# Wide and narrow products of a two-layer decoder trunk in another order, with later attention steps and squares on VectorE in the tail

## The chip, the cores and the metric

One core of a Trainium2 chip runs the kernel. The time is device time in microseconds (us) of one execution, and the reported number is the median of several executions: before the change 838.62 us, of three runs from 836.81 to 839.08.

Engines are named as in the profile: PE is TensorE (PEld its weight loads), DVE is VectorE, ACT is ScalarE, POOL is GpSimd, SP is SyncE, which here only issues DMAs.

## What is computed

Two decoder layers on 256 tokens of width 2048, in fp32. Layer 0 mixes tokens by forgetting attention (FoX, 32 heads of 64, a learned decay added to the logits), layer 1 by sliding-window attention with grouped keys, learned sinks and partial rotation. Each layer projects the normalised input to q, k, v and a gate, multiplies the attention output by silu(gate), projects back and adds the residual. A last RMSNorm ends it.

```python
def reference(x, norm_g, fox_w_in, fox_b_f, fox_w_out, swa_w_in, swa_sinks, swa_w_out, final_g):
    ...
    for i in range(DEPTH):
        h = rmsnorm(x, norm_g[i])
        j = i // N_MIXERS
        if i % N_MIXERS == 0:
            p = h @ fox_w_in[j]
            ...
            y = fox_attention(q, k, v, log_f)
            w_out = fox_w_out[j]
        else:
            p = h @ swa_w_in[j]
            ...
            y = swa_attention(q, k, v, swa_sinks[j])
            w_out = swa_w_out[j]
        y = y * jax.nn.silu(gate)
        x = x + y @ w_out
    return rmsnorm(x, final_g)
```

## The kernel before

**Products.** Every operand of a projection is split into a high part (rounded to fp32r) and a low part (the rest). For weights this is a cast on ACT (L218) and a subtract on DVE (L219), four k-tiles of 128 rows at a time. A projection's 256 output columns are a `Unit`; its 16 k-tiles come in *parts* of four, and each part is worked in two blocks, one for each half `c` of the output columns (or of the tokens, for a `v` unit). A block of four k-tiles is four *wide* matmuls (high weights held, high and low activations moved together, 512 columns) and then four *narrow* ones (low weights held, high activations moved, 256 columns). Both add into the PSUM tile `acc`, whose two halves ACT (L282, a copy of the second) and DVE add together when the unit is finished. That is the unit's `consume`: for q and k it also scales and splits (`q` L513, L514, L342, L343; `k` L519, L520, L524 to L528), for the gate it goes on to silu (L308, L309, L296 to L303).

**Order.** PE's instructions stay in program order. The loop at the end of `trunk` goes through the stream of all parts, and each iteration runs block 0 of this part and then block 1 of the part before. Weights are fetched by SP three parts ahead into raw buffers, and the cast of a part waits until one of the five `w` buffers is free, which is when the last matmul that uses it is done.

**Attention by steps.** After every second matmul of a block `tick()` counts a step, eight in an iteration, and runs what is due then. The attention of a finished group is hung on these steps by `attend`, counted from when its `k` (or, in layer 1, its `q`) is consumed. A FoX group has two pairs of heads. For each pair: at `s - BIAS` the bias is asked for (a DMA by POOL, L567, and POOL's `affine_select`, L126), at step `s` comes a first score product (`ps_s`, keys of both blocks) with its bias add and reduction on DVE (L378, L365), at `s + SECOND` the second product (the first block of queries; `s_first`, L390, L365) and the softmax: two small operations on DVE (L579, L580), four exponentials on ACT (L321), reciprocal and four multiplies on DVE (L329, L332). At step `t` and `t + 4` PE transposes the two heads' weights (`pt`, L82), and at a last step come the products with `v` (`psy`). The score tiles share one PSUM buffer (`ps_s`, one buffer), so a score product waits until the reduction of the one before is done.

The steps stand in five tables: `FOX_FIRST` for group 0, `FOX_NEXT` for group 1, `FOX_ODD` for groups 3 and 5, `FOX_DUE` for 2, 4, 6 and 7, and `SWA_DUE` for the eight groups of layer 1. After an even FoX group's `k` come its gate (consumed 32 steps later), the next group's `q` (64 steps) and `k` (96). Odd groups have a `v` unit for two groups there, in 512 columns.

**Tail.** The last projection is worked half by half of the tokens; `finish` adds the residual, takes the sum of squares of the last two column blocks, works out the scale, spreads it over the partitions by a matmul with a diagonal matrix (`rows`), multiplies (L754) and sends the output in five pieces.

Of the kernel before, what the change touches and what calls it, by code (L numbers as in the profile page):

```python
# [48 lines left out]
KBUFS = 1  # L49
# [8 lines left out]
def trunk(  # L58
# [19 lines left out]
    def mm(*args, **kw):  # L78
        tc.keep_in_program_order(nc.tensor.matmul(*args, **kw))  # L79
# [142 lines left out]
    def block(unit, p, c):  # L222
        _, _, _, kt0, s = unit.parts[p]
        w, a = loaded[unit, p], unit.acts
        if p == 0 and (c == 0 or unit.apart):

            pool, tag, banks = unit.apart if c == 1 else (*unit.acc, 2)
            ps = pool.tile([P, banks, 512], F32, tag=tag, name="acc")
            if unit.apart:
                unit.ps[c] = ps[:, 0, :]  # L230
            else:
                unit.ps, unit.both = [ps[:, i, :] for i in range(2)], ps
        n = unit.n if unit.kind == "tok" else S
# [10 lines left out]
        ops = [operands(i) for i in range(s)]  # L244
        if unit.halves:

            for i, (sh, _, mv) in enumerate(ops):
                mm(both, sh, mv.rearrange("p h n -> p (h n)"), start=first and i == 0, stop=False)
                if i % 2:
                    tick()  # L250
            if s % 2:
                tick()
            for i, (_, sl, mv) in enumerate(ops):
                mm(ps, sl, mv[:, 0, :], start=False, stop=last and i == s - 1)
                if i % 2:
                    tick()
        elif n == 512:
            for i, (sh, sl, mv) in enumerate(ops):
                mm(ps, sh, mv[:, 0, :], start=first and i == 0, stop=False)
                mm(ps, sh, mv[:, 1, :], start=False, stop=False)  # L260
                tick()
                mm(ps, sl, mv[:, 0, :], start=False, stop=last and i == s - 1)
                tick()
        else:
            for i, (sh, sl, mv) in enumerate(ops):
                mm(ps, sh, mv[:, 0, :], start=first and i == 0, stop=False)
                mm(ps, sl, mv[:, 0, :], start=False, stop=False)
            for i, (sh, _, mv) in enumerate(ops):
                mm(ps, sh, mv[:, 1, :], start=False, stop=last and i == s - 1)
                tick()  # L270
        if p == len(unit.parts) - 1:
            if unit.apart:
                unit.consume(c, both)
            elif c == 1 and unit.kind == "tok":
                for i in range(2):
                    unit.consume(i, unit.ps[i])
            elif c == 1:
                unit.consume(unit.both)

    def low_half(ps):  # L280
        s = work.tile([P, 2, S], F32, tag="half", name="half", bufs=HALVES)
# [64 lines left out]
    class Pair:  # L346
# [92 lines left out]
    class Group:  # L439


        def attend(self, kt, due, shared):
            self.pts = [None, None]
            for j, (s, t, *second) in enumerate(due[0:2]):
                self.pair(j).later(self, s, t, *(second or [SECOND]))
            after(due[2], lambda: self.values(kt, shared))

        def values(self, kt, shared):
# [218 lines left out]
    def to_layer1(m):  # L667
        split_x(m, 1)
        square_into(sums1, m)
        if m == KT - 1:  # L670

            def norm():
                nonlocal swa
                fox_scope.__exit__(None, None, None)
                swa = ctx.enter_context(tc.tile_pool(name="swa", bufs=2))
                state["r1"] = r = inv_rms(
                    sums1, "n1", True, ps_s.tile([P, 2, 512], F32, tag="S", name="ps_n1")[:, 0, :]
                )
# [43 lines left out]
    def finish(th, ps):  # L722
# [2 lines left out]
        nc.vector.tensor_add(x, ps[:, 0 : 2 * P], x)  # L725
# [4 lines left out]
        nc.scalar.activation(sq, x, AF.Square, accum_out=ss)  # L730
        nc.scalar.activation(r, ss, AF.Ln, scale=1.0 / D, bias=tail["ss"][:, th : th + 1])
        nc.scalar.activation(r, r, AF.Exp, scale=-0.5)
        nc.vector.tensor_scalar(
            v, ss, 1.0 / D, tail["ss"][:, th : th + 1], op0=ALU.mult, op1=ALU.add
        )

        nc.vector.scalar_tensor_tensor(out=w, in0=r, scalar=-0.5, in1=r, op0=ALU.mult, op1=ALU.mult)
        nc.scalar.activation(diag, ident, AF.Copy, scale=r)
        nc.vector.tensor_scalar(w, w, v, 1.5, op0=ALU.mult, op1=ALU.add)
        nc.vector.tensor_scalar_mul(diag, diag, w)  # L740
        nc.vector.tensor_mul(r, r, w)

        def scale():
            rows = ps_s.tile([P, 2, 512], F32, tag="S", name="rows")[:, 0, :]
# [188 lines left out]
    sink = cpool.tile([P, H], F32, name="sink")  # L933
    state["sink"] = sink

    prev = None
    for i, (u, p) in enumerate(stream):
        fetch(i + 1 + LOOK)
        if u is last_out[7]:
            if p == 0:  # L940
                block(*prev, 1)
            block(u, p, 0)
            continue
        block(u, p, 0)
        if prev is not None:
            block(*prev, 1)
        prev = (u, p)
    for p in range(len(last_out[7].parts)):
        block(last_out[7], p, 1)


# ---- launch: one core; the host only lays arrays out
# [62 lines left out]
```

## Time and profile before

| | before |
|---|---|
| median of 3 runs | 838.62 us |
| the profiled execution | 838.05 us |
| its span | 836.3 us |
| mean granted PE clock | 0.995 |
| instructions in the span | 12770 |
| HBM traffic | 147.50 MB read, 2.15 MB written |

The profiled execution's own time is 1.75 us more than its span, which goes from the first to the last instruction on record. The profile's page gives busy time for each engine; matmuls are pipelined, so a busy PE only says that there was always a matmul in its pipe. The waits view names, for each engine, what the instruction waited for that ended an idle time; the chain is followed back from the last instruction; the timeline lists instructions by start time (us from the start of the span), with the idle time before them and its releaser in brackets.

### The profile page before, as it was taken

To read this page: it belongs to the slowest core of one execution; us is meant where nothing else is said; L and a number is where in the kernel's file an instruction comes from. 1 tells how busy PE (TensorE), PEld (TensorE's weight loads), DVE (VectorE), ACT (ScalarE), POOL (GpSimd) and SP (SyncE) were. 2 spreads that over 40 slices of the span, in tenths; PEclk is the share of its full clock that TensorE was granted. 3 is DMA by queue.
4 is the path that set the end of the run, shared out by engine and by line. 5 is a ranking of instruction groups with operands and counts; after the bars stand their busy time and mean duration, and the time that the engine had idled before them with its cause. 6 is when DMAs were issued, how large, how long until landed. Compare 5 with 4: busy or idle time off the path is not lost.

```text
span 836.3 us, 12770 instructions
## 1 busy us (share of the span) xinstructions
PE 822.7 (98%) x4778; PEld 708.7 (85%) x4778; DVE 644.8 (77%) x1201; ACT 519.6 (62%) x936; POOL 60.9 (7%) x93
## 2 busy tenths in 40 slices
PE   8999999999999999999999999999999999999995
PEld 7888788888888888888888888888888888888885
DVE  6898866887679866798659768788998888875654
ACT  6686665764666665576646556477667766765552
POOL 1011010010101010020002110000000000001210
PEclk9999999999999999999999999999999999999998
DMA  8667564555646555554374564544455435346622
GB/s 281 241 229 246 173 207 164 185 206 170 212 160 196 185 199 188 172 188 171 130 251 164 198 201 158 196 159 152 144 170 181 151 120 185 115 142 207 205 95 102
DMA packets 28399, 150.48 MB, mean 180 GB/s; under 512 B 3457, under 2 KB 5665, under 8 KB 14513
## 3 DMA queue, kind: packets, MB, share of 16 engines
q1 hardware_dynamic: 25920, 142.22, 50.0%
q0 software_dynamic: 1408, 6.36, 2.1%
q10 hardware_dynamic: 1008, 1.07, 0.4%
q8 instruction: 38, 0.62, 0.3%
q14 instruction: 25, 0.20, 0.1%
HBM read 147.50 MB, written 2.15 MB: 179 GB/s over the span
## 4 chain that ended last, share of the span: by engine, by line
PE 90%; DVE 4%; issue 3%; ACT 1%; DMA 1%; SPq 0%; POOL 0%; DVEq 0%; ACTq 0%; POOLq 0%
PE acc L79 82%; PE ps_s L79 3%; PE pt L82 2%; PE psy L79 2%; DVE w L219 1%; DVE q L343 1%; ACT w L218 1%; DMA wraw<-in_vf_dram 1%; SPq L210 0%; DVE xs L160 0%; DVE ys L462 0%; ACT st L321 0%; DVE st L365 0%; DVE scaled L754 0%; DVE st L332 0%
## 5 line engine op out<-in xcount | busy, mean ns | idle before, releaser
L79 PE MATMUL acc<-xs,w 128*128 128x256 f32 (+1 forms) x2624 | 485.6, 340 | 0.1
L79 PEld LDWEIGHTS acc<-xs,w 128*128 128x128 f32 x2624 | 406.8, 189 | 59.8 <-issue 3.4
L219 DVE TENSOR_TENSOR w<-wraw,w 128x1024 fp32r<-128x1024 f32 (+4 forms) x275 | 326.0, 1191 | 97.2 <-ACT w L218 95.1
L218 ACT CAST w<-wraw 128x1024 fp32r<-128x1024 f32 (+4 forms) x275 | 278.4, 1016 | 146.6 <-PE acc L79 107.0
L79 PE MATMUL acc<-ys,w 128*128 128x512 f32 x960 | 171.4, 338 | 0.0
L79 PEld LDWEIGHTS acc<-ys,w 128*128 128x128 f32 x960 | 147.6, 189 | 21.5 <-issue 0.4
L79 PE MATMUL acc<-w,xs 128*128 128x512 f32 (+2 forms) x512 | 111.4, 364 | 1.6 <-ACT w L218 1.3
L79 PEld LDWEIGHTS acc<-w,xs 128*128 128x128 f32 x512 | 86.8, 189 | 16.0 <-ACT w L218 1.6
L282 ACT COPY half<-acc 128x512 f32<-128x512 f32 x56 | 32.7, 583 | 81.4 <-PE acc L79 81.0
L321 ACT ACTIVATE st<-st,mx 128x128 f32<-128x128 f32 (+1 forms) x128 | 56.6, 445 | 2.4 <-DVE mx L827 1.6
L401 ACT COPY pts<-pt 128x384 f32<-128x384 f32 x64 | 30.4, 475 | 13.7 <-PE pt L82 12.9
L332 DVE TENSOR_SCALAR st<-st,rl 128x128 f32<-128x128 f32 (+1 forms) x128 | 32.9, 321 | 1.1
L79 PE MATMUL ps_s<-kk,q 128*128 128x256 f32 (+1 forms) x160 | 32.0, 310 | 1.8 <-DVE mx L365 1.1
L82 PE MATMUL pt<-ident,st 128*128 128x128 f32 x192 | 31.9, 274 | 0.3 <-DVE st L332 0.3
L661 POOL TENSOR_TENSOR acc<-acc,sq 128x256 f32<-128x256 f32 x28 | 24.5, 875 | 88.6 <-ACT sq L655 87.5
L365 DVE CUSTOM_DVE_ANT_0 st<-ps_s,st 128x128 f32<-128x128 f32 (+1 forms) x96 | 28.3, 331 | 1.1
L82 PEld LDWEIGHTS pt<-ident,st 128*128 128x128 f32 x192 | 23.5, 140 | 6.4 <-ACT half L282 0.7
L126 POOL TENSOR_SCALAR_AFFINE_SELECT bc<-bc 128x256 f32<-128x256 f32 x32 | 22.0, 706 | 74.6 <-DMA bc<-negc_d 74.6
L79 PEld LDWEIGHTS ps_s<-kk,q 128*128 128x128 f32 x160 | 23.4, 188 | 4.2 <-issue 1.5
L659 POOL COPY acc<-sq 128x256 f32<-128x256 f32 x2 | 1.3, 672 | 329.8 <-ACT sq L655 329.8
L567 POOL DMA_DIRECT2D bc<-negc_d x16 | 8.8, 553 | 213.7 <-DVE mx L365 186.3
L321 ACT ACTIVATION_READ_ACCUMULATOR st<-st,mx 128x1 f32 x128 | 24.2, 189 | 0.0
(139 smaller groups left out, 530.4 us busy)
## 6 DMA issues: line engine op xcount, KB each, us to landing
wraw<-in_fox_in_dram SPq DMA_DIRECT2D x46, 1024.0 KB, 5.0
wraw<-in_swa_in_dram SPq DMA_DIRECT2D x36, 1024.0 KB, 5.0
wraw<-in_fox_in_dram SPq DMA_DIRECT2D x28, 512.0 KB, 4.8
wraw<-in_fox_out_dram SPq DMA_DIRECT2D x13, 1024.0 KB, 5.0
wraw<-in_swa_out_dram SPq DMA_DIRECT2D x13, 1024.0 KB, 5.1
bc<-negc_d POOLq DMA_DIRECT2D x16, 384.0 KB, 5.3
wraw<-in_fox_out_dram SPq DMA_DIRECT2D x6, 512.0 KB, 3.6
wraw<-in_swa_out_dram SPq DMA_DIRECT2D x6, 512.0 KB, 3.6
```

The lines of the kernel that those rows point to most:

```text
L79: tc.keep_in_program_order(nc.tensor.matmul(*args, **kw))
L82: tc.keep_in_program_order(nc.tensor.transpose(out, in_, ident))
L126: return nc.gpsimd.affine_select(out=ap, in_=ap, compare_op=ALU.is_ge, fill=NEG, base=base, pattern=pattern, channel_multiplier=mult,)
L218: state["split"] = nc.scalar.copy(high, raw)
L219: nc.vector.tensor_tensor(out=low, in0=raw, in1=high.bitcast(F32), op=ALU.subtract)
L282: nc.scalar.copy(s, ps[:, :, S : 2 * S])
L321: nc.scalar.activation(st[:, hh, rng], st[:, hh, rng], AF.Exp, bias=nm[:, qb, hh : hh + 1], accum_out=l[:, qb, hh : hh + 1],)
L332: nc.vector.tensor_scalar_mul(st[:, hh, rng], st[:, hh, rng], rl[:, qb, hh : hh + 1])
L365: nc.vector.tensor_tensor_reduce(out=st, in0=high, in1=st, scale=self.scale, scalar=LOWEST, op0=ALU.add, op1=ALU.max, accum_out=self.mx[:, ...
L401: nc.scalar.copy(group.pts[hh][:, self.j, :], pt[:, 0 : 3 * P])
L567: nc.gpsimd.dma_start(out=bc, in_=negc_d[h0 : h0 + 2, :].partition_broadcast(P))
L661: nc.gpsimd.tensor_add(sums[0], sums[0], s)
```

## The change

Four things are changed.

1. `block` issues the wide matmuls at once and returns a function that issues the narrow ones (and then the `consume` of a finished unit). An iteration now runs: wide of this part's block 0, wide of the part before's block 1, narrow of the part before's block 1, narrow of this part's block 0. Wide and narrow ones thus come in runs of eight.
2. The tables of steps: scores 2 to 4 steps later, transposes 3 to 6 and values 4 to 5 steps later; `SECOND` from 10 to 12 (in `FOX_FIRST` from 12 to 14). The first pair of group 0 asks for its bias 26 steps ahead of its scores, not `BIAS` = 14.
3. The layer's `norm` comes at step 20, not 16.
4. In `finish` the sum of squares goes from ACT (Square with accumulation) to DVE (multiply and reduce in one), the diagonal is made by one DVE operation from `r` and `w`, without ACT's copy, the multiply by `g` comes last, and the output pieces are 3, 4, 4, 2 and 1 blocks, not 2, 4, 4, 2 and 2.

```diff
-FOX_DUE = ((18, 46), (50, 76), 106)
-FOX_ODD = ((18, 46), (50, 76), 116)
-FOX_FIRST = ((50, 82, 12), (70, 98), 116)
-FOX_NEXT = ((26, 54), (56, 86), 116)
-SWA_DUE = ((28, 52), (47, 69), 79)
-
-SECOND = 10
+FOX_DUE = ((20, 50), (52, 80), 110)
+FOX_ODD = ((20, 50), (52, 80), 120)
+FOX_FIRST = ((54, 88, 14, 26), (74, 104), 120)
+FOX_NEXT = ((28, 58), (58, 90), 120)
+SWA_DUE = ((31, 57), (50, 74), 84)
+
+SECOND = 12
...
+        def narrow():
+            for i, (_, sl, mv) in enumerate(ops):
+                mm(ps, sl, mv[:, 0, :], start=False, stop=last and i == s - 1)
+                if i % 2:
+                    tick()
+            done()
+
         if unit.halves:
 
             for i, (sh, _, mv) in enumerate(ops):
...
             if s % 2:
                 tick()
-            for i, (_, sl, mv) in enumerate(ops):
-                mm(ps, sl, mv[:, 0, :], start=False, stop=last and i == s - 1)
-                if i % 2:
-                    tick()
-        elif n == 512:
+            return narrow
+        if n == 512:
...
-        def later(self, group, s, t, second):
+        def later(self, group, s, t, second=SECOND, bias=BIAS):
             self.second = second
-            after(s - BIAS, self.early)
+            after(s - bias, self.early)
...
-            after(16, norm)
+            after(20, norm)
...
-        nc.vector.tensor_mul(xg, x, tail["g"])
         ss, v, r, w = (work.tile([P, 1], F32, tag=f"tail{i}", name=f"tail{i}") for i in range(4))
-        nc.scalar.activation(sq, x, AF.Square, accum_out=ss)
-        nc.scalar.activation(r, ss, AF.Ln, scale=1.0 / D, bias=tail["ss"][:, th : th + 1])
-        nc.scalar.activation(r, r, AF.Exp, scale=-0.5)
+        nc.vector.tensor_tensor_reduce(
+            out=sq, in0=x, in1=x, scale=1.0, scalar=0.0, op0=ALU.mult, op1=ALU.add, accum_out=ss
+        )
...
-        nc.scalar.activation(diag, ident, AF.Copy, scale=r)
         nc.vector.tensor_scalar(w, w, v, 1.5, op0=ALU.mult, op1=ALU.add)
-        nc.vector.tensor_scalar_mul(diag, diag, w)
+        nc.vector.tensor_scalar(diag, ident, r, w, op0=ALU.mult, op1=ALU.mult)
         nc.vector.tensor_mul(r, r, w)
+        nc.vector.tensor_mul(xg, x, tail["g"])
...
-            for i, n in enumerate((2, 4, 4, 2, 2)):
+            for i, n in enumerate((3, 4, 4, 2, 1)):
...
-        block(u, p, 0)
+        narrow = block(u, p, 0)
         if prev is not None:
-            block(*prev, 1)
+            block(*prev, 1)()
+        narrow()
         prev = (u, p)
```

Line numbers move by 8 to 12; L321, L329, L332, L365 and L390 of before are L330, L338, L341, L374 and L399 now, L282 is L291, L342 and L343 are L351 and L352, L513 and L514 are L522 and L523, L579 and L580 are L588 and L589.

On PE, around pair 1 of group 2 (`q_1411` holds its queries before, `q_1407` after), the program had before:

```order
L79 MATMUL acc<-xs,w 128x256 x4
L79 MATMUL ps_s<-kk,q_1411 128x256 x2
L79 MATMUL acc<-xs,w 128x512 x4
L79 MATMUL acc<-xs,w 128x256 x4
L79 MATMUL acc<-xs,w 128x512 x4
L79 MATMUL acc<-xs,w 128x256 x4
```

and now:

```order
L79 MATMUL acc<-xs,w 128x256 x4
L79 MATMUL ps_s<-kk,q_1407 128x256 x2
L79 MATMUL acc<-xs,w 128x256 x4
L79 MATMUL acc<-xs,w 128x512 x8
L79 MATMUL acc<-xs,w 128x256 x8
L79 MATMUL acc<-xs,w 128x512 x8
L79 MATMUL acc<-xs,w 128x256 x4
L82 MATMUL pt<-ident,st 128x128 x3
```

The runs of four have become runs of eight, and the second score product stands in the middle of a run of narrow ones, where the next group's `q` has just been finished.

On ACT, the same place, from the copy of the half of the next group's `q` on. Before:

```order
L282 COPY half<-acc 128x512
L218 CAST w<-wraw 128x2x512
L321 ACTIVATE st,l<-st,mx 128x128
L321 ACTIVATE st,l<-st,mx 128x256
L321 ACTIVATE st,l<-st,mx 128x128
L321 ACTIVATE st,l<-st,mx 128x256
L342 CAST q_1773<-q 64x2x256 x2
L218 CAST w<-wraw 128x2x512
```

Now:

```order
L291 COPY half<-acc 128x512
L218 CAST w<-wraw 128x2x512
L351 CAST q_1769<-q 64x2x256 x2
L218 CAST w<-wraw 128x2x512
L330 ACTIVATE st,l<-st,mx 128x128
L330 ACTIVATE st,l<-st,mx 128x256
L330 ACTIVATE st,l<-st,mx 128x128
L330 ACTIVATE st,l<-st,mx 128x256
L218 CAST w<-wraw 128x2x512
```

The four exponentials now stand behind the casts of the next `q` and a second cast of weights.

On DVE, the same place, from the second product's bias add. Before:

```order
L390 TENSOR_TENSOR st<-ps_s,bc 128x2x128
L365 ISA st,mx<-ps_s,st 128x128
L365 ISA mx 128x1
L365 ISA st,mx<-ps_s,st 128x128
L365 ISA mx 128x1
L579 TENSOR_TENSOR mx<-mx,cq 128x4
L580 TENSOR_TENSOR mx<-cq,mx 128x4
L513 TENSOR_TENSOR q<-acc,half 128x512
L514 TENSOR_TENSOR q<-q,r_492 128x512
L219 TENSOR_TENSOR w<-wraw,w 128x2x512
L329 RECIPROCAL rl<-l 128x4
```

Now:

```order
L399 TENSOR_TENSOR st<-ps_s,bc 128x2x128
L522 TENSOR_TENSOR q<-acc,half 128x512
L374 ISA st,mx<-ps_s,st 128x128
L374 ISA mx 128x1
L374 ISA st,mx<-ps_s,st 128x128
L374 ISA mx 128x1
L523 TENSOR_TENSOR q<-q,r_492 128x512
L588 TENSOR_TENSOR mx<-mx,cq 128x4
L219 TENSOR_TENSOR w<-wraw,w 128x2x512
L589 TENSOR_TENSOR mx<-cq,mx 128x4
L352 TENSOR_TENSOR q_1769<-q,q_1769 64x2x256 x2
L219 TENSOR_TENSOR w<-wraw,w 128x2x512
```

The two operations of the next `q` have moved in between those of the softmax, and a subtract of weights has moved ahead of the last of them.

More of the change, by code (lines that the diff above doesn't have):

```diff
@@ L244, in block, with done @@
         ops = [operands(i) for i in range(s)]
+        def done():
+            if p < len(unit.parts) - 1:
+                return
+            if unit.apart:
+                unit.consume(c, both)
+            elif c == 1 and unit.kind == "tok":
+                for i in range(2):
+                    unit.consume(i, unit.ps[i])
+            elif c == 1:
+                unit.consume(unit.both)
+        def narrow():
[4 more added lines that the diff above has]
+            done()
         if unit.halves:
@@ L270, in block @@
                 tick()
[L271 to L278, printed above, removed]
+        done()
+        return lambda: None
     def low_half(ps):
@@ L443, in attend @@
             self.pts = [None, None]
-            for j, (s, t, *second) in enumerate(due[0:2]):
-                self.pair(j).later(self, s, t, *(second or [SECOND]))
+            for j, steps in enumerate(due[0:2]):
+                self.pair(j).later(self, *steps)
             after(due[2], lambda: self.values(kt, shared))
@@ L735, in finish @@
         )
+        nc.scalar.activation(r, ss, AF.Ln, scale=1.0 / D, bias=tail["ss"][:, th : th + 1])
+        nc.scalar.activation(r, r, AF.Exp, scale=-0.5)
         nc.vector.scalar_tensor_tensor(out=w, in0=r, scalar=-0.5, in1=r, op0=ALU.mult, op1=ALU.mult)
-        nc.scalar.activation(diag, ident, AF.Copy, scale=r)
         nc.vector.tensor_scalar(w, w, v, 1.5, op0=ALU.mult, op1=ALU.add)
-        nc.vector.tensor_scalar_mul(diag, diag, w)
+        nc.vector.tensor_scalar(diag, ident, r, w, op0=ALU.mult, op1=ALU.mult)
         nc.vector.tensor_mul(r, r, w)
+        nc.vector.tensor_mul(xg, x, tail["g"])
         def scale():
@@ L940, in trunk @@
             if p == 0:
-                block(*prev, 1)
-            block(u, p, 0)
+                block(*prev, 1)()
+            block(u, p, 0)()
             continue
-        block(u, p, 0)
+        narrow = block(u, p, 0)
         if prev is not None:
-            block(*prev, 1)
+            block(*prev, 1)()
+        narrow()
         prev = (u, p)
     for p in range(len(last_out[7].parts)):
-        block(last_out[7], p, 1)
+        block(last_out[7], p, 1)()
 def _units(w, n, per):
```

## Prediction

> **What bounds the kernel now.** I read the page's first two sections first, then the chain of work that ended last by line, then the waits of TensorE (PE), then the timeline around each place that the change touches. The page:
>
> ```profile
> PE 822.7 (98%) x4778; PEld 708.7 (85%) x4778; DVE 644.8 (77%) x1201; ACT 519.6 (62%) x936; POOL 60.9 (7%) x93
> ...
> PE 90%; DVE 4%; issue 3%; ACT 1%; DMA 1%; SPq 0%; POOL 0%; DVEq 0%; ACTq 0%; POOLq 0%
> ...
> L79 PE MATMUL acc<-xs,w 128*128 128x256 f32 (+1 forms) x2624 | 485.6, 340 | 0.1
> ...
> L79 PE MATMUL acc<-ys,w 128*128 128x512 f32 x960 | 171.4, 338 | 0.0
> ```
>
> PE is busy 98% of the span, and 90% of the chain is its own. The last two rows are the products in question, 2624 + 960, half wide and half narrow. So only two things can move the end: how far apart PE's matmuls start, and how long PE stands still. All the standing still that the trace records between matmuls:
>
> ```profile
> PE rows L79 <- DVE tail L741: 2.5, 1, 2.5
> PE acc L79 <- ACT w L218: 1.3, 1, 1.3
> PE ps_s L79 <- DVE mx L365: 1.1, 1, 1.1
> PE warm L79 <- DVE ones L119: 1.1, 1, 1.1
> PE ps_s L79 <- DVE q L343: 0.7, 4, 0.2
> PE pt L82 <- DVE st L332: 0.3, 1, 0.3
> PE acc L79 <- DVE w L219: 0.3, 1, 0.3
> ```
>
> The columns are total us, number, longest. The sum is 7.3 us. Of these the change can reach the third (1.1), the fifth (0.7), the sixth (0.3) and a little of the first (2.5). The others belong to the start (data not there yet), where no instruction is moved.
>
> **Term 1, the order of wide and narrow products.** Nothing is added: (2624 + 960)/2 = 1792 wide matmuls and as many narrow ones stay. The only price is the distance from start to start. Pieces of the chain, as start, length, what, number of matmuls:
>
> ```profile
> 96.09 3.40 PE acc L79 x15
> 99.72 6.15 PE acc L79 x27
> ...
> 422.44 80.66 PE acc L79 x460
> ...
> 823.93 2.89 PE acc L79 x24
> ```
>
> The third is the four-wide, four-narrow alternation: 80.66/460 = 175.3 ns, or 350.7 for a wide one and a narrow one. The first two are long stretches of wide ones alone, 3.40/15 = 226.7 and 6.15/27 = 227.8 ns; the last are narrow ones alone, 2.89/24 = 120.4. A pair in long runs would cost 347.1, so the alternation pays 3.6 ns a pair, 14.4 ns for every four and four. Were that a fixed price of each run, eight and eight would halve it: 7.2 ns for every four pairs, 1792/4 times, is 3.2 us. At best all of it goes, 3.6 x 1792 = 6.5 us. No row shows a longer run that is dearer for each matmul, so the other end is nothing. A run of eight is nearer to four than to fifteen; I take **-2.0 us**.
>
> The Trainium skill ("TensorE: Matmul & The Clock Gate", section "Back-to-back issue gap") gives the distance of isolated matmuls as N/2.4 + 2.5 ns, which holds nothing on the length of a run. By that rule this term is 0 and the sum below 846.1; the trace's 226.7 ns against the rule's 216 for 512 columns says that it does not describe this kernel closely.
>
> **Term 2, waits that go.** In the eight groups of the second layer the first scores now come 3 steps later (28 to 31), and an iteration of eight steps takes 16 x 175.3 = 2.81 us, so each gets about 1.0 us more. The longest of the four waits for `q` L343 is 0.2, so all 0.7 go: **-0.7**. In the tail, the last half's chain before the matmul that waits 2.5:
>
> ```profile
> 827.30 0.42 ACT L730 ACTIVATE rest<-tail_x 128x256 f32<-128x256 f32 x1 [3.89 <-DVE tail_x L725]
> ...
> 827.62 0.19 ACT L730 ACTIVATION_READ_ACCUMULATOR rest<-tail_x 128x1 f32 x1
> ...
> 828.40 0.40 ACT L738 ACTIVATE rest<-ident,tail 128x128 f32<-128x128 f32 x1
> ...
> 828.92 0.29 DVE L740 TENSOR_SCALAR rest<-rest,tail 128x128 f32<-128x128 f32 x1
> ```
>
> The square and its sum take 0.51 on ACT (827.30 to 827.81). On VectorE (DVE) the nearest row, the add and reduction in one of L365 on the same 128x256 (168.59, below), takes 0.42: -0.1. L738 leaves, and L740 no longer waits for it, -0.1. The moved multiply by `g` runs behind, beside PE. Between -0.4 (both in full) and +0.2 (the multiply of 0.42 delays the row output), **-0.2**. The sum of output bytes is unchanged.
>
> **Term 3, the first attention group.**
>
> ```profile
> 54.21 0.53 POOL L487 DMA_DIRECT2D negc_d<-once  x1 [50.42 <-DVE once L486]
> ...
> 59.76 1.10 POOL L567 DMA_DIRECT2D bc<-negc_d  x2 [4.53 <-ACT w L218]
> ...
> 67.15 0.76 POOL L126 TENSOR_SCALAR_AFFINE_SELECT bc<-bc 128x256 f32<-128x256 f32 x2 [6.29 <-DMA bc<-negc_d]
> 67.94 0.69 DVE L378 TENSOR_TENSOR st<-ps_s,bc 128x512 f32<-128x512 f32 x1 [2.11 <-POOL bc L126]
> ...
> 70.07 0.47 PE L79 MATMUL ps_s<-kk,q 128*128 128x256 f32 x2 [1.12 <-DVE mx L365]
> ...
> 84.54 0.80 PE L82 MATMUL pt<-ident,st 128*128 128x128 f32 x3 [0.28 <-DVE st L332]
> ```
>
> The bias is now asked for 26 steps ahead of its scores, not 14, but its DMA reads what `forget` writes to memory (issued at 54.21), and POOL has stood idle for 4.53 by 59.76. The row names a cast as what ended this, of whose result the DMA reads nothing; I put it down to the write. POOL's order is unchanged, so the bias lands no sooner and the select still ends near 67.9; SP's order of loads is unchanged there too. What helps is the second product, due 6 steps later (50+12 to 54+14): it is now wanted near 70.2, when the reduction is done, and 1.1 goes. But the next pair's product follows 6 steps behind instead of 8, and needs the same PSUM buffer back. Between lie on DVE the next group's `q` (two of 0.69), a subtract (1.22) and the bias add and reduction (about 1.0): with 0.4 for the product from 70.2, and some of the `q` done before it, the buffer is free near 73.9 and wanted near 72.4. So 1.5 comes, and the 0.3 at `pt` stays: about **+0.1** net, from -1.4 (everything goes) to +0.6.
>
> **Term 4, groups 2, 4 and 6.** Here I expect the time to be lost. Pair 1 of group 2:
>
> ```profile
> 168.59 0.42 DVE L365 CUSTOM_DVE_ANT_0 st<-ps_s,st 128x256 f32<-128x256 f32 x1
> ...
> 169.34 0.40 PE L79 MATMUL ps_s<-kk,q 128*128 128x256 f32 x2
> ...
> 171.18 0.59 ACT L282 COPY half<-acc 128x512 f32<-128x512 f32 x1 [1.98 <-PE acc L79]
> ...
> 171.66 1.05 ACT L218 CAST w<-wraw 128x1024 fp32r<-128x1024 f32 x1
> ...
> 171.79 0.69 DVE L513 TENSOR_TENSOR q<-acc,half 128x512 f32<-128x512 f32 x1
> ...
> 172.61 0.40 ACT L321 ACTIVATE st<-st,mx 128x128 f32<-128x128 f32 x1
> ...
> 173.13 1.22 DVE L219 TENSOR_TENSOR w<-wraw,w 128x1024 fp32r<-128x1024 f32 x1
> ...
> 174.38 1.25 ACT L342 CAST q<-q 64x512 fp32r<-64x512 f32 x2
> 174.50 0.18 DVE L329 RECIPROCAL rl<-l 128x4 f32<-128x4 f32 x1 [0.15 <-ACT st L321]
> ...
> 175.19 0.58 PE L82 MATMUL pt<-ident,st 128*128 128x128 f32 x3
> ```
>
> Before, the second product stood at step 60, the next `q` was finished at 64, and the exponentials began 172.61 - 169.34 = 3.27 after the product, ahead of the casts of `q`. The transposes came 5.85 after the product and 2.58 after the first exponential (175.19 - 172.61), with PE held for a moment (0.58 for three, where others take 0.49). Nothing was in hand.
>
> Now the product stands at step 64, where `q` is finished, and ACT's order is: copy of the half, cast, both casts of `q`, cast, and then the exponentials. Busy time alone is 0.59 + 1.05 + 1.25 + 1.05 = 3.94. With waits: the half starts 0.2 after the product; DVE adds the bias from 0.45, then two 0.69 of `q` with the reduction between them end near 2.8; the casts of `q` run to 4.1, the second weight cast to 5.1. The exponentials start at about 5.05, so the transposes can start 2.58 later, at 7.63. PE wants them 16 steps after the product, 2 x 2.81 + 0.24 = 5.86. Wait **1.8**; by ACT's busy time alone (start at 4.1) 0.8; with DVE's queue 0.3 behind, 2.1.
>
> Pair 0 of the same groups moves from 28 to 32, where the gate is finished:
>
> ```profile
> 156.78 0.40 PE L79 MATMUL ps_s<-kk,q 128*128 128x256 f32 x2
> ...
> 160.05 0.40 ACT L321 ACTIVATE st<-st,mx 128x128 f32<-128x128 f32 x1
> ...
> 161.81 0.62 ACT L296 ACTIVATE gate_e<-gt 128x512 f32<-128x512 f32 x1
> ...
> 163.56 0.49 PE L82 MATMUL pt<-ident,st 128*128 128x128 f32 x3
> ```
>
> The exponentials again started 3.27 after the product, and the transposes came 6.78 after it, 0.9 in hand. Now ACT has half, cast, the gate's first function (L296, which needs the multiply L309 on DVE, done near 2.85) and a cast ahead: start near 4.45, transposes possible at 7.03, wanted at 6.3 (the 18 steps after the product are now two iterations, four narrow matmuls and the product itself, 2 x 2.81 + 4 x 0.12 + 0.24). Wait **0.7**; from 0 (busy time alone, 0.59 + 1.05 + 0.62 + 1.05 = 3.3, is ready at 6.0) to 1.0. While PE stands nothing else is done, since every later matmul is behind it in its queue. Three groups: 3 x (1.8 + 0.7) = 7.5, less what pair 1 lost already (3 x 0.1): **+7.2**, from 2.1 to 9.
>
> Group 7 has the same steps with its `v` in place of `q` (no casts of `q` on ACT): 0.7 + 0.9 = **+1.6**, from 0 to 2. In groups 1, 3 and 5 nothing is finished beside pair 0, and beside pair 1 only a `v` of two groups, whose scalings go ahead of the exponentials: of the 0.9 that pair 0 had in hand above some stays, 0; were it gone, the price is that of group 7 for each.
>
> **Sum**, against the profiled 838.05 (median 838.62 lies 0.57 above, inside the spread of the runs 836.81 to 839.08, and isn't added): 838.05 - 2.0 - 0.7 - 0.2 + 0.1 + 7.2 + 1.6 = **844.1**.
>
> **Rivals.**
> - *The softmax keeps pace.* No new wait in the groups, and the old ones go: 838.05 - 2.0 - 0.9 - 1.4 - 0.3 = 833.5, faster. It decides at an exponential of pair 1 that starts within 5.86 - 2.58 = 3.28 of its product. ACT's 3.94 of work ahead of it speaks against; that two of the engines run below 80% speaks for slack. Chance 0.13.
> - *Wide runs of eight reach 226.7 at once*, and the waits are only those of busy time: 838.05 - 6.5 - 0.9 + 0.1 + 2.1 = 832.9 at the extreme, and with the waits as summed 839.6; the lone stretches are at that rate, but they have no narrow ones between them. Chance 0.10, mostly as no change.
> - *Only pair 1 waits*, pair 0's 0.9 in hand holding: 844.1 - 3 x 0.7 - 1.6 = 840.4. Chance 0.14, no change or just slower.
> - *The second layer waits too.* Its transposes come 26 and 24 steps after the scores, and a gate or a `q` finished beside them takes the ACT at 8 x 2 places; at 0.25 each 844.1 + 4 = 848.1. The waits of before show none there. Chance 0.08.
> - *The grouping doesn't do what it says* (term 1 nothing): 844.1 + 2.0 = 846.1. Chance 0.10, counted with the forecast, in whose own range it lies.
>
> **How the numbers follow.** The forecast has 0.55, with an own range of 841.5 to 847. A measurement of this kernel can tell about 0.3% (2.5 us) from no change. Faster by more: 0.15 (the first rival and the extreme of the second). Within: 0.19. Slower by more: 0.66. The range reaches to the second and third rivals and to the bounds of term 4 above: 837.5 to 848.
>
> **What would show it.** Right: waits of PE for `st` of L341 (once L332) at the transposes, some six to eight, 0.7 to 2 long, in groups 2, 4, 6 and 7; the first exponential of pair 1 some 5 us behind its product, both casts of `q` ahead of it; a wait of about 1.5 for `mx` at the third score product of the first group; no wait for `q` in the second layer; long pieces of the chain at 174 to 175 ns a matmul. Wrong: pieces at 173.5 (term 1 larger), or no waits for `st` at all (term 4 gone).

## The result, and the profile after

The changed kernel takes 844.33 us (median of 6 runs, 843.73 to 845.36) against 838.02 for the one before (6 runs, 836.81 to 839.08): a ratio of 1.0077, 95% interval 1.0066 to 1.0088. It is slower by 6.3 us. The profiled execution took 844.93, of which the page shows a span of 843.2:

```profile
span 843.2 us, 12766 instructions
...
PE 822.8 (98%) x4778; PEld 709.7 (84%) x4778; DVE 641.4 (76%) x1205; ACT 520.2 (62%) x930; POOL 54.7 (6%) x93
...
PE 89%; DVE 4%; ACT 3%; issue 2%; DMA 1%; SPq 0%; DVEq 0%; ACTq 0%
```

No engine does more work than before: the busy times agree within 1% on PE, DVE and ACT. What has changed is the chain, where ACT now has 3%, not 1%. The waits view of PE says where (total us, number, longest):

```profile
PE pt L82 <- DVE st L341: 7.0, 9, 1.5
PE rows L79 <- DVE rest L749: 2.5, 1, 2.5
PE warm L79 <- DVE ones L119: 1.1, 1, 1.1
PE acc L79 <- ACT w L218: 0.7, 1, 0.7
PE ps_s L79 <- DVE mx L374: 0.6, 1, 0.6
PE acc L79 <- DVE w L219: 0.2, 1, 0.2
```

The row for the transposes was 0.3 in one wait and is 7.0 in nine. The waits for `q` in layer 1 (0.7) are gone. Pair 1 of group 2, in the timeline:

```profile
170.23 0.40 PE L79 MATMUL ps_s<-kk,q 128*128 128x256 f32 x2
...
170.43 0.59 ACT L291 COPY half<-acc 128x512 f32<-128x512 f32 x1 [1.32 <-PE acc L79]
...
170.91 1.06 ACT L218 CAST w<-wraw 128x1024 fp32r<-128x1024 f32 x1
...
172.07 0.69 DVE L523 TENSOR_TENSOR q<-q,r 128x512 f32<-128x512 f32 x1
...
172.85 1.26 ACT L351 CAST q<-q 64x512 fp32r<-64x512 f32 x2 [0.88 <-DVE mx L588]
173.89 0.15 DVE L589 TENSOR_TENSOR mx<-cq,mx 128x4 f32<-128x4 f32 x1
...
174.14 1.05 ACT L218 CAST w<-wraw 128x1024 fp32r<-128x1024 f32 x1
175.10 0.39 ACT L330 ACTIVATE st<-st,mx 128x128 f32<-128x128 f32 x1
...
177.75 0.78 PE L82 MATMUL pt<-ident,st 128*128 128x128 f32 x3 [1.53 <-DVE st L341]
```

Read it down from the product at 170.23. ACT copies the half, casts weights, stands for 0.88 until DVE has finished the next `q` (L523, to 172.76; the row names L588, the short operation behind it, but the cast reads only `q`), casts that `q` and casts weights again. Only at 175.10, 4.87 after the product, does the first exponential start, although the numbers it needs (L589) were there at 174.04. These were late themselves: 3.81 after the product, against 2.39 before the change (L580, to 171.73), since DVE now has the two operations of `q` and a subtract of weights ahead of the last of them. The same operation before the change:

```profile
171.56 0.17 DVE L580 TENSOR_TENSOR mx<-cq,mx 128x4 f32<-128x4 f32 x1
```

In the changed kernel PE stands 1.53 and then takes 0.78 for three transposes that take 0.49 where nothing holds them: the weight loads of the second and third start only at 178.09, after PEld has stood 0.23 for their multiplies (L341). Pair 0 of the same group:

```profile
156.94 0.40 PE L79 MATMUL ps_s<-kk,q 128*128 128x256 f32 x2
...
159.51 0.63 ACT L305 ACTIVATE gate_e<-gt 128x512 f32<-128x512 f32 x1 [0.83 <-DVE gt L318]
...
160.23 1.05 ACT L218 CAST w<-wraw 128x1024 fp32r<-128x1024 f32 x1
...
161.19 0.40 ACT L330 ACTIVATE st<-st,mx 128x128 f32<-128x128 f32 x1
...
163.64 0.85 PE L82 MATMUL pt<-ident,st 128*128 128x128 f32 x3 [0.23 <-DVE st L341]
```

Here the exponentials start 4.25 after the product, behind the gate's first function and a cast; PE stands 0.23 and loses another 0.36 inside the three transposes.

One long piece of the chain, the third of those shown before, has become shorter:

```profile
431.68 80.30 PE acc L79 x460
```

That is 174.6 ns a matmul against 175.3, 2793 ns an iteration of sixteen against 2805.

The table puts the profiles of all runs side by side. M250 and Mlast are the starts, in the trace, of matmul 250 of the projections (counted from 0) and of the last one; the start of a kernel, the part between and the tail come apart that way. Each row's profile is of one execution. Times are us.

| kernel | ratio to before | M250 | Mlast | between | Mlast to end of span |
|---|---|---|---|---|---|
| before | 1 | 49.21 | 826.52 | 777.31 | 9.75 |
| changed | 1.0077 (1.0066 to 1.0088) | 49.11 | 832.17 | 783.06 | 10.98 |
| grouping_alone | 1.0006 (0.9997 to 1.0016) | 50.57 | 826.02 | 775.45 | 9.74 |
| steps_alone | 1.0085 (1.0070 to 1.0101) | 49.57 | 832.95 | 783.38 | 9.62 |
| product_ahead | 0.9975 (0.9965 to 0.9986) | 50.91 | 824.26 | 773.35 | 9.36 |
| transposes_later | 0.9971 (0.9959 to 0.9982) | 50.52 | 823.76 | 773.24 | 9.38 |
| one_step_ahead | 1.0042 (1.0029 to 1.0055) | 49.77 | 830.34 | 780.57 | 9.38 |
| product_ahead_again | 0.9966 (0.9955 to 0.9978) | 50.30 | 824.33 | 774.03 | 9.36 |
| start_as_before | 0.9974 (0.9965 to 0.9982) | 50.01 | 823.48 | 773.47 | 9.36 |
| old_tail | 0.9971 (0.9961 to 0.9982) | 51.18 | 824.81 | 773.63 | 9.75 |
| old_order_fixed_steps | 0.9993 (0.9984 to 1.0002) | 49.77 | 825.82 | 776.05 | 9.42 |
| first_group_later | 0.9947 (0.9934 to 0.9959) | 50.31 | 822.58 | 772.27 | 9.40 |

### The profile page after: what moved, and what is told of

Read it like the earlier page. It is cut to its first block, busy times and chain, and to the rows that moved or that the text cites. A ratio compares the mean times of both kernels' runs of the same rounds, so it can differ in the third digit from the quotient of the medians.

```text
span 843.2 us, 12766 instructions
## 1 busy us (share of the span) xinstructions
PE 822.8 (98%) x4778; PEld 709.7 (84%) x4778; DVE 641.4 (76%) x1205; ACT 520.2 (62%) x930; POOL 54.7 (6%) x93
## 4 chain that ended last, share of the span: by engine, by line
PE 89%; DVE 4%; ACT 3%; issue 2%; DMA 1%; SPq 0%; DVEq 0%; ACTq 0%
PE acc L79 80%; PE psy L79 3%; PE pt L82 3%; PE ps_s L79 3%; ACT st L330 2%; DMA wraw<-in_vf_dram 1%; DVE w L219 1%; DVE st L341 1%; ACT w L218 1%; DMA wraw<-in_fox_in_dram 0%; ACT q L351 0%; DVE xs L160 0%; DVE q L522 0%; SPq L210 0%; DVE st L374 0%
## 5 line engine op out<-in xcount | busy, mean ns | idle before, releaser
L79 PE MATMUL acc<-ys,w 128*128 128x256 f32 (+1 forms) x960 | 170.6, 338 | 0.0
L291 ACT COPY half<-acc 128x512 f32<-128x512 f32 x56 | 32.7, 584 | 70.3 <-PE acc L79 69.9
L330 ACT ACTIVATE st<-st,mx 128x128 f32<-128x128 f32 (+1 forms) x128 | 56.8, 446 | 8.0 <-DVE mx L589 8.0
L341 DVE TENSOR_SCALAR st<-st,rl 128x128 f32<-128x128 f32 (+1 forms) x128 | 34.3, 331 | 1.1
L374 DVE CUSTOM_DVE_ANT_0 st<-ps_s,st 128x128 f32<-128x128 f32 (+1 forms) x96 | 28.2, 332 | 0.8
L330 ACT ACTIVATION_READ_ACCUMULATOR st<-st,mx 128x1 f32 x128 | 24.2, 189 | 0.0
L160 DVE SCALAR_TENSOR_TENSOR xs<-xT,g_sb,xs 128x256 fp32r<-128x256 f32 x32 | 20.5, 680 | 3.7 <-ACT xs L159 3.7
```

The costliest lines, as they stand in the source:

```text
L160: nc.vector.scalar_tensor_tensor(out=xs[:, kt, 1, :], in0=xT[:, kt, :], scalar=g, in1=xs[:, kt, 0, :].bitcast(F32), op0=ALU.mult, op1=ALU. ...
L291: nc.scalar.copy(s, ps[:, :, S : 2 * S])
L330: nc.scalar.activation(st[:, hh, rng], st[:, hh, rng], AF.Exp, bias=nm[:, qb, hh : hh + 1], accum_out=l[:, qb, hh : hh + 1],)
L341: nc.vector.tensor_scalar_mul(st[:, hh, rng], st[:, hh, rng], rl[:, qb, hh : hh + 1])
L374: nc.vector.tensor_tensor_reduce(out=st, in0=high, in1=st, scale=self.scale, scalar=LOWEST, op0=ALU.add, op1=ALU.max, accum_out=self.mx[:, ...
```

## The experiments

### Which part makes the waits

Theory A is the prediction's: the new steps put the second product on the step at which a unit is finished, so ACT has that unit's work and the casts ahead of the exponentials. Theory B is that the grouping itself does it. (Over all tables the transposes come 4 to 6 steps later; the list of the change says 3 to 6.) First the grouping by itself, with the tables, the norm's step and the tail of before:

```diff
 # the changed kernel, with
+FOX_DUE = ((18, 46), (50, 76), 106)
+FOX_ODD = ((18, 46), (50, 76), 116)
+FOX_FIRST = ((50, 82, 12), (70, 98), 116)
+FOX_NEXT = ((26, 54), (56, 86), 116)
+SWA_DUE = ((28, 52), (47, 69), 79)
+SECOND = 10
...
+            after(16, norm)
```

> The new order of wide and narrow matmuls alone; the step tables, the norm's step and the tail are those of before. Theory A (the new steps put the second score product on the step at which a unit is finished, so that ACT takes the casts of that unit ahead of the exponentials; the grouping is innocent): no wait of PE for st at the transposes of groups 2, 4 and 6 over 0.3 us, eight wide and eight narrow matmuls start within 2793 ns as in the changed kernel (2805 before), 224 iterations, so about 2.5 us faster than before: near 835.5, ratio 0.997. Rival B (the grouping makes the waits: narrow steps are shorter, and weights are given back at another moment): waits of 1 us or more at the transposes of groups 2, 4 and 6, 841 or more.

Measured: 838.16 against 837.23, a ratio of 1.0006. No wait for `st` in groups 2 to 7, so the grouping is innocent of the loss. But the gain that theory A forecast is not in the time: 0.997 lies outside the interval. In the profile the part from M250 to Mlast is 1.9 us shorter, and the start 1.4 us later. PE still waits 0.7 for `q` in layer 1, and 1.0 (0.3 before) at the transposes of group 0.

Then the steps by themselves, with the order and the tail of before:

```diff
 # the kernel before, with
+FOX_DUE = ((20, 50), (52, 80), 110)
+FOX_ODD = ((20, 50), (52, 80), 120)
+FOX_FIRST = ((54, 88, 14, 26), (74, 104), 120)
+FOX_NEXT = ((28, 58), (58, 90), 120)
+SWA_DUE = ((31, 57), (50, 74), 84)
+SECOND = 12
...
+            after(20, norm)
```

> The new step tables and the norm at step 20, with the order of wide and narrow matmuls and the tail of before. Theory A: the exponentials of pair 1 in groups 2, 4 and 6 start about 4.9 us behind their product, as in the changed kernel (before: 3.3), PE waits about 1.6 at each of these transposes and up to 0.5 at those of pair 0 and of group 7; the four waits for q in the second layer are gone: near 843, ratio 1.006. Rival B: no such waits, 837 to 838.

Measured: 844.68, 1.0085 (the forecast of 1.006 lies below the interval). The steps alone cost all that the whole change costs. The waits view, and pair 1 of group 2 in the timeline:

```profile
PE pt L82 <- DVE st L332: 6.3, 5, 1.6
...
171.95 0.40 PE L79 MATMUL ps_s<-kk,q 128*128 128x256 f32 x2
...
174.57 1.26 ACT L342 CAST q<-q 64x512 fp32r<-64x512 f32 x2 [0.89 <-DVE mx L579]
...
176.81 0.40 ACT L321 ACTIVATE st<-st,mx 128x128 f32<-128x128 f32 x1
...
179.52 0.78 PE L82 MATMUL pt<-ident,st 128*128 128x128 f32 x3 [1.56 <-DVE st L332]
```

The exponentials start 4.86 behind their product with matmuls in fours as well. Theory B falls. Of the five waits three are pair 1 of groups 2, 4 and 6 (1.56, 1.39, 1.39), one is in group 7 (0.73) and one in group 0 (1.25). At pair 0 no wait is listed, though the three transposes are still held inside (0.62 to 0.87 in place of 0.49). An iteration that begins with four wide matmuls leaves pair 0 about 0.5 us more: with the products at their old steps, its transposes come 8.20 after the product in the old order (old_order_fixed_steps) and 7.70 in the new one (product_ahead).

### Product and transposes, moved one at a time

```diff
-FOX_DUE = ((20, 50), (52, 80), 110)
+FOX_DUE = ((18, 50, 10), (50, 80, 10), 110)
```

> The changed kernel with one table altered: in FOX_DUE (groups 2, 4, 6, 7) the scores come at 18 and 50 and the second product 10 steps later, at 28 and 60 as before; transposes (50, 80) and values stay as changed. Theory A: the four exponentials are ahead of the casts of q in ACT's order again and start about 3.3 us behind their product; no wait at the transposes of these groups, about 7.7 us less than the changed kernel: near 836.5, ratio 0.998. Rival B: waits as in the changed kernel, 843 or more.

Measured: 835.17, 0.9975; the same kernel run again gave 834.56, 0.9966. The place in group 2:

```profile
169.90 0.40 PE L79 MATMUL ps_s<-kk,q 128*128 128x256 f32 x2
...
172.11 0.16 DVE L589 TENSOR_TENSOR mx<-cq,mx 128x4 f32<-128x4 f32 x1
...
173.17 0.41 ACT L330 ACTIVATE st<-st,mx 128x128 f32<-128x128 f32 x1
...
174.94 1.25 ACT L351 CAST q<-q 64x512 fp32r<-64x512 f32 x2
...
177.12 0.49 PE L82 MATMUL pt<-ident,st 128*128 128x128 f32 x3
```

The casts of `q` are behind the exponentials again, these start 3.27 after the product as they did before the change, and the transposes take their 0.49. DVE's order is the old one here too: the numbers for the exponentials (L589) are ready 2.37 after the product, not 3.81, so this run moves both orders at once. The products of one table, the second ones four steps sooner and the first ones two, are worth 8.6 to 9.3 us in the ratios (0.0102 to 0.0111 of 838).

```diff
-FOX_DUE = ((20, 50), (52, 80), 110)
+FOX_DUE = ((20, 54), (52, 86), 116)
```

> The changed kernel with one table altered: in FOX_DUE the transposes come 4 and 6 steps later (54 and 86) and the values at 116; the second products stay on steps 32 and 64. Theory A: the exponentials start as late as in the changed kernel (4.9 us behind the product in pair 1), but PE now has 1.4 and 2.1 us more of other work before it needs them, against waits of 0.5 and 1.7: nearly all waits at the transposes go, near 837, ratio 0.9985. Rival C (PE loses the time because ACT and DVE as a whole have too much to do around these steps): the waits move to a later place of the same group, 841 or more.

Measured: 835.25, 0.9971, a little below the forecast 0.9985. The order on ACT and DVE is the bad one still, and it does not matter:

```profile
170.87 0.40 PE L79 MATMUL ps_s<-kk,q 128*128 128x256 f32 x2
...
175.73 0.40 ACT L330 ACTIVATE st<-st,mx 128x128 f32<-128x128 f32 x1
...
179.03 0.49 PE L82 MATMUL pt<-ident,st 128*128 128x128 f32 x3
```

The exponentials start 4.86 behind the product, the transposes stand 8.16 behind it, and PE has other products in between. So the loss is neither a lack of speed on ACT nor the order on ACT and DVE by itself. It is that order against the distance that the table leaves, and either end can be moved. Rival C falls, since nothing came back later in the group.

```diff
-FOX_DUE = ((20, 50), (52, 80), 110)
+FOX_DUE = ((20, 50, 11), (52, 80, 11), 110)
```

> The changed kernel with FOX_DUE's second product one step earlier (31 and 63, not 32 and 64), all else as changed. ACT's order then has the exponentials behind the half, and two casts of weights, but ahead of the casts of q and of the gate's first function. Theory A, by ACT's order: the second cast waits for its buffer until about 3.5 behind the product, so the exponentials start 4.2 to 4.6 behind it and not 4.9; the transposes are wanted one narrow step later after the product; PE waits about 0.8 to 1.1 in pair 1 and 0.2 to 0.5 in pair 0 of groups 2, 4, 6: near 840, between the changed kernel and product_ahead. Rival (only the casts of q matter): no waits at the transposes, near 836.

Measured: 841.16, 1.0042, 2.9 us better than the change (0.0035 of 838), 5.6 to 6.4 worse than product_ahead and about 1 above the forecast. In the profile PE waits 2.0 for `mx` in group 0, where it waited 0.6 in the changed kernel, and the table moved here is not that of group 0. In pair 1:

```profile
171.90 0.40 PE L79 MATMUL ps_s<-kk,q 128*128 128x256 f32 x2
...
175.29 0.16 DVE L589 TENSOR_TENSOR mx<-cq,mx 128x4 f32<-128x4 f32 x1
...
175.37 1.05 ACT L218 CAST w<-wraw 128x1024 fp32r<-128x1024 f32 x1 [1.26 <-PE acc L79]
...
176.32 0.40 ACT L330 ACTIVATE st<-st,mx 128x128 f32<-128x128 f32 x1
...
178.87 0.61 PE L82 MATMUL pt<-ident,st 128*128 128x128 f32 x3 [0.74 <-DVE st L341]
```

With the casts of `q` behind them the exponentials still start 4.42 after the product. ACT stands 1.26 in front of the second cast of weights, until PE gives back a buffer, and everything behind that cast stands with it. The numbers for the exponentials were ready at 175.45, 3.55 after the product, so the cast accounts for the last 0.87; what is ahead of that is DVE's queue, where a subtract of weights still stands ahead of L589. So the casts of `q` are only part of the price; a cast that waits for PE is another, and by these rows DVE's order is a third. The rival, which had only the casts of `q`, falls.

### What the grouping is worth, and the start

For the start, two runs on one chip with the second run of product_ahead, whose expectation was:

> The kernel of product_ahead again, as the base for the two after it on the same chip. Both theories: the same steady part as before (from matmul 250 of the projections to the last one about 4.0 us less than in the kernel before), ratio 0.997 to 0.998. Theory D (the new order costs about 1.5 us in the first 45 us, while weights still arrive): matmul 250 starts at 50.5 or later, as in grouping_alone, product_ahead and transposes_later (50.5 to 50.9; 49.2 before and 49.1 in the changed kernel's own profile). Rival E (the start differs by chance from execution to execution): anything from 49 to 51.

```diff
         narrow = block(u, p, 0)
+        if i < len(start):
+            narrow()
         if prev is not None:
             block(*prev, 1)()
-        narrow()
+        if i >= len(start):
+            narrow()
```

> The kernel of product_ahead, with the old order (a block's narrow matmuls right behind its wide ones) for the 24 parts of the start and the new order from there on. Theory D: matmul 250 starts near 49.3 and the kernel is 1 to 1.5 us faster than product_ahead_again: ratio to before about 0.996. Rival E: same as product_ahead_again within 0.5 us, and a start that is not earlier in the mean.

Measured: 835.33, 0.9974 (0.9965 to 0.9982), against 0.9966 (0.9955 to 0.9978). It is not faster. (The list `start` in the kernel has 23 parts, not 24.) Its profile has matmul 250 at 50.01, 0.3 earlier than product_ahead_again; theory D wanted 49.3. It is not borne out. Over all profiles M250 lies from 49.1 to 51.2 with the new order in the start (eight profiles, mean 50.3) and from 49.2 to 50.0 with the old one (four, mean 49.6); one profile for each kernel doesn't settle whether a small difference is there.

Then the grouping beside good tables, taken out of product_ahead:

```diff
-        narrow = block(u, p, 0)
+        block(u, p, 0)()
         if prev is not None:
             block(*prev, 1)()
-        narrow()
```

> The kernel of product_ahead (new tables with FOX_DUE's products at 28 and 60, new norm step, new tail), with the old order of wide and narrow matmuls. What the grouping alone is worth beside the same tables. If an iteration of 2793 against 2805 ns counts in full, this is 224 x 0.012 = 2.7 us slower than product_ahead (834.6 to 835.2), near 837.5, ratio 1.000. If the grouping is worth nothing in the time, as grouping_alone's ratio of 1.0006 suggests, it is as fast as product_ahead: ratio 0.997.

Measured: 837.31, 0.9993 (0.9984 to 1.0002), so the grouping is worth 0.0018 to 0.0027, or 1.5 to 2.3 us; the intervals of the ratios just touch, and the traces bear it out. Between M250 and Mlast it is 776.05 against 773.35 and 774.03: 2.0 to 2.7. That includes the waits of group 0, which differ from execution to execution; from matmul 600 on, behind group 0, it is 1.8. The 12 ns of an iteration (2805 to 2793), 224 times, are 2.7, so most of it reaches the time. It is worth less with the tables of before (grouping_alone).

### The tail

```diff
 # product_ahead, with finish() of the kernel before
+        nc.vector.tensor_mul(xg, x, tail["g"])
...
+        nc.scalar.activation(sq, x, AF.Square, accum_out=ss)
...
+        nc.scalar.activation(diag, ident, AF.Copy, scale=r)
...
+            for i, n in enumerate((2, 4, 4, 2, 2)):
```

> The kernel of product_ahead with the tail of before (square on ACT, diagonal in two operations, pieces 2, 4, 4, 2, 2). From the last matmul of the projections to the end of the span: 9.8 us as in the kernel before, against 9.34 in product_ahead; so 0.45 slower than product_ahead_again if the tail change is what shortened it, and the 11.0 of the changed kernel's own profile was a slow landing of output DMAs in that execution. Rival: the new tail is the slower one in the mean (its last DMAs collide), and this kernel is 0.5 to 1 us faster than product_ahead_again.

Measured: 834.93, 0.9971 (0.9961 to 0.9982), which the times can't tell from product_ahead. In the profiles the last matmul of the projections stands 9.74 to 9.75 ahead of the end with the old tail (three profiles; 9.62 in steps_alone) and 9.36 to 9.42 with the new one (seven profiles). The eighth, the changed kernel's own, has 10.98. Its tail before the output was as quick as in the others:

```profile
832.95 0.43 DVE L738 CUSTOM_DVE_ANT_0 rest<-tail_x 128x256 f32<-128x256 f32 x1
...
834.42 0.34 DVE L749 TENSOR_SCALAR rest<-ident,tail,tail 128x128 f32<-128x128 f32 x1
...
834.91 0.46 PE L79 MATMUL rows<-rest,ones 128*128 128x128 f32 x2 [2.46 <-DVE rest L749]
...
835.41 2.28 DVE L764 TENSOR_TENSOR scaled<-xT,rows 128x384 f32<-128x384 f32 x5 [0.45 <-PE rows L79]
```

but its output took longer to land. From the DMA view of its last 10 us (the last number is us from issue to landing), and then the same row of product_ahead:

```profile
out_dram<-scaled SPq DMA_DIRECT2D x1, 256.0 KB, 4.1
```

```profile
out_dram<-scaled SPq DMA_DIRECT2D x1, 256.0 KB, 2.1
```

The other seven profiles of the new tail land as product_ahead's does, so the slow landing is a matter of that execution, not of the new tail. What caused it is open.

### The first group, and a faster kernel

The waits left in product_ahead that a table can reach are those of group 0. In the changed kernel:

```profile
59.44 1.10 POOL L576 DMA_DIRECT2D bc<-negc_d  x2 [4.41 <-DMA negc_d<-once]
65.32 1.29 POOL L126 TENSOR_SCALAR_AFFINE_SELECT bc<-bc 128x256 f32<-128x256 f32 x2 [4.78 <-DMA bc<-negc_d]
...
72.94 0.70 PE L79 MATMUL ps_s<-kk,q 128*128 128x512 f32 x2 [0.59 <-DVE mx L374]
...
85.54 0.61 PE L82 MATMUL pt<-ident,st 128*128 128x128 f32 x3 [0.57 <-DVE st L341]
```

```diff
 # product_ahead, with
-FOX_FIRST = ((54, 88, 14, 26), (74, 104), 120)
+FOX_FIRST = ((54, 90, 14, 26), (76, 108), 124)
```

> The kernel of product_ahead with FOX_FIRST at ((54, 90, 14, 26), (76, 108), 124): in group 0 the second pair's scores come 8 steps behind the first pair's second product as before the change, not 6, and the transposes 2 and 4 steps later. The wait of PE for mx at the third score product of group 0 (0.6 to 1.5 in five profiles of the new tables) falls below 0.3 and the wait for st at the transposes of group 0 (0.3 to 0.6) goes: 1 us faster than product_ahead, ratio to before near 0.9955. If group 0's waits are fed by the late bias instead, they come back at the next product and the time stays.

Measured: 833.76 against 838.02, 0.9947 (0.9934 to 0.9959), 4.3 us faster than the kernel before in the medians and the lowest ratio of all. Both waits of group 0 are gone from its waits view. Its lead over the two runs of product_ahead (0.9975 and 0.9966) is 1.6 to 2.3 us, more than the 1 forecast; the part from M250 to Mlast gives 1.1 to 1.8.

## Why the prediction was right

844.1 was forecast and 844.33 measured. The mechanism is the one forecast: the second products meet the end of a unit, the exponentials start late, and PE stands at the transposes of groups 2, 4, 6 and 7. That the sum came within 0.3 is partly luck, since single terms are off by up to 0.9, in both directions.

Behind group 0 the traces of one kernel repeat themselves (product_ahead and product_ahead_again agree within 0.1 us from matmul 600 to the last), so that two kernels can be compared by the starts of the same matmul.

- **Term 4 and group 7** (7.2 + 1.6 = 8.8). The time of the change less that of product_ahead is 8.6 to 9.3 us. The start of the exponentials was put at 5.05 behind the product in pair 1 and at 4.45 in pair 0; the trace of group 2 has 4.87 and 4.25. Both were forecast 0.2 too late; DVE's queue was a little quicker than assumed. What the waits view counts as standing (1.53, 1.50, 1.42 and 0.23, 0.33, 0.46 in groups 2, 4, 6, and 0.23 and 0.75 in group 7) is not all, and for pair 0 it is below the 0.7 named as a sign: held transposes also take 0.6 to 0.87 for three in place of 0.49, and a wait counts only from the modelled end of the matmul before. By starts against product_ahead, PE loses 2.7, 2.6 and 2.8 in groups 2, 4 and 6 and 1.6 in group 7, 9.7 in all. Some 0.3 of that was lost before the change too (0.58 for three transposes), so it is 9.4 against the forecast 8.8: groups 2, 4 and 6 were put 0.6 too low, group 7 was right. (Its 0.9 for pair 1 stands in the forecast without a working; the trace has 1.0.) No wait came in groups 1, 3 and 5.
- **Term 1** (-2.0). Measured -1.5 to -2.3 in the time beside good tables, 2.0 to 2.7 in the trace, 1.8 of it behind group 0. The value between nothing and the halved price of a run was the right one, and the runs differ by length, 2793 against 2805 ns an iteration. The rule that the prediction weighed (the Trainium skill, "TensorE: Matmul & The Clock Gate", section "Back-to-back issue gap"), in which the length of a run has no part, would have it at 0 and is not borne out by this trace.
- **Term 2** (-0.7 and -0.2). The waits for `q` are gone from the changed kernel and stay where the old tables stay, but their price was put at less than half. From matmul 2700 to the last, in layer 1, the kernel before takes 293.3 us and steps_alone 291.7: -1.6. At each of the four places two starts that follow at 120 and 118 ns elsewhere follow at about 440 and 220, which is 0.42 lost, while the view lists 0.16, from the modelled end of the matmul before. The tail gave -0.4 in seven profiles, at the edge of its bounds; in the changed kernel's own profile the slow landing hid it, which made this one execution 1.2 longer there.
- **Term 3** (+0.1). The wait of 1.1 went and came back one product later, as said, but at 0.6 in this execution, where 1.5 was forecast; others have up to 2.0, and old_order_fixed_steps lists none there. The one at the transposes grew from 0.3 to 0.6. The bias came no sooner for being asked for sooner: POOL issued its DMA at 59.44 (59.76 before), and the releaser is now named, the write of `negc_d`. Net -0.2 in this execution.
- **The rivals.** That the softmax keeps pace fell, as did waits in layer 1 and pair 1 alone waiting. Wide runs of eight do not reach 227 ns at once: the first five take 228 to 236 (below). The mechanism of the first rival was sound as a remedy, however: with the exponentials 3.27 behind the product, where it said that the case decides, the kernel is 0.9966 to 0.9975.

Two causes inside term 4 go beyond the prediction. With the casts of `q` out of the way, the cast that waits for PE's buffer still holds the exponentials to 4.42 (one_step_ahead); the prediction had this cast in its sum, but not that it is enough to make PE wait. And DVE's order alone makes the numbers for the exponentials 3.81 late: had ACT been free then, the transposes could have followed some 2.55 later, at about 6.4 (an estimate from the rows), still behind the 5.86 at which the prediction has PE want them. No run moves DVE's order without ACT's, so how the loss divides between the two is not shown.

Not settled either is why the grouping with the old tables shows nothing in the time while its trace is 1.9 us shorter from M250 to Mlast.

## What to carry to other kernels

When a schedule hangs small work on the steps of a large loop, write down for each engine what stands between the two ends of the small chain, by its order and not by its busy share: here ACT was busy for 62% of the span and still 1.6 us late, because the exponentials stood behind casts that waited for other engines, those of `q` for DVE (0.88) and, in one_step_ahead, one of weights for PE (1.26), which then waited for the exponentials. Moving both ends by the same number of steps is not neutral if one of them moves past the point where another unit is finished. And price a wait by the distance between starts, not by what the waits view lists: in layer 1 the list had 0.7 where 1.6 was to be gained. And where two edits are made together, time each alone with tables that suit it: the gain of the grouping and the loss of the steps came as one number of the wrong sign.

## What was not expected of the hardware

The price of changing between wide and narrow matmuls isn't a step at the change. Median distances from start to start in undisturbed iterations (ns; more than a hundred iterations of each kernel):

```
before   wide  235 234 236 226   narrow 117 120 120 120   wide  233 235 229 232   narrow 117 119 118 117
changed  wide  233 236 228 233 231 227 227 227             narrow 113 119 120 120 120 120 120 120
```

The first five wide ones of a run of eight cost 228 to 236 and the later ones 227, while the narrow ones settle at 120 from 113 to 119: by these medians an iteration with runs of eight saves 18 ns on the wide side and gives back 4 on the narrow one (by means 16 and 4, the 12 of the iteration). Starts of whole executions also vary more than expected, matmul 250 from 49.1 to 51.2 us, and the last six output DMAs landed in 1.7 to 2.3 us in all profiles but one, and in 3.0 to 4.1 in that one.
